# The order of the projection jobs in a streaming encoder layer

## The chip, the cores and the metric

The kernel runs as one program on 1 core of one Trainium2 chip. The metric is the device time of one execution in microseconds (us). A core has five engines that each work through a list of instructions of their own, in the order in which the list was written: PE (TensorE, matrix products), ACT (ScalarE), DVE (VectorE), POOL (GpSimd) and SP (SyncE, which in this kernel only issues DMAs). An instruction waits on semaphores until those before it on other engines, or the DMAs that it needs, are done. PEld is the loading of PE's stationary operand, which overlaps the products.

## The reference

One layer of an encoder is computed for a prompt of 2048 frames and for 64 further frames of a running stream. The layer normalizes its input of width 1024, projects it with one matrix of 4096 columns, and cuts the product into eight features of width 512:

```python
aq, ak, av, ag, hq, hf, hi, hg = jnp.split(rms_norm(x, ln_g) @ w_in, SPLITS, axis=-1)
o_a = attn_fn(heads(aq), k, v).reshape(B, T, W_A) * jax.nn.silu(ag)
o_b, S = hgrn2_branch(hq, hf, hi, hg, lb, norm_g, s0)
y = x + jnp.concatenate([o_a, o_b], axis=-1) @ w_out
```

Group A is attention over 8 heads of width 64 (query, key, value and gate: aq, ak, av, ag); each chunk of 64 frames sees itself and the 8 chunks before it. Group B is a gated linear recurrence over 4 heads of width 128 (forget gate, query, input and output gate: hf, hq, hi, hg). Keys, values and recurrent states are outputs too, and a last RMSNorm follows.

## The kernel before, in words

**Tiles and stages.** The 2112 frames are cut into four super-blocks (SUPER): 512 frames, then 512 and the 64 running ones, then 512 and 512. For each one, x is normalized and transposed into two tiles, xh (rounded) and xl (the rest), so that a product of full precision is three products of rounded operands: w's rounded part with xh, with xl, and w's rest with xh. The eight heads of group A are worked as four pairs.

**The projections are jobs.** A job is a feature of a pair or of a recurrent head: ("pq", 2) is the query of pair 2, ("hg", 0) the gate of recurrent head 0. Each super-block has 32 jobs of 128 columns of w_in; project() runs one as 24 matmuls per block of frames into one of two PSUM banks (acc), and starts an evacuation (ev_q, ev_k, ev_v or ev_v_last, ev_f, ev_i, or silu_to for the gates and the recurrent query) that brings the bank into SBUF on ACT and DVE and gives it free. The table JOBS names the order in which the main program runs the jobs, and the list `order` made from it is the order in which weights() loads their columns. The first two and the last two jobs of a super-block run in halves of the frames (x's second half can still be on its way when the first two begin). When eight jobs are left, the x tiles of the next super-block are started, or in the last super-block the loads for the output projection.

**What else is on PE.** As soon as its features are there, a pair's attention and a head's recurrence run beside the jobs of others. Attention goes s (scores, one PSUM bank), pr (softmax on DVE and ACT), tr (transposed back on PE, two banks), ph (tr split into a rounded part by ACT at L951 and a rest by DVE at L954), pv (product with the values), mixa (times the gate on POOL, L1095). A recurrence runs in one PSUM bank, g. After the last job, the steps of the output projection (out_step) fill PE; out_parts() cuts their left operands into slot, xh and xl tiles, by a copy on ACT (L1687) and a difference on POOL or DVE (L1695).

**What sets the order.** All five instruction lists are written by the Python class Plan. Every piece of work is a generator that yields what it waits for; Plan keeps a clock of its own, and whichever piece is ready first writes its instructions next. On the chip the lists are fixed: an instruction whose data are late holds up everything behind it on its engine. Buffers are counted by tokens (Tok): two for sig (staging of gates, of new key and value rows that go to the output, and of loads), three for vT (staging of query, key, value, input), two for sga (gates of pairs).

**Lines that the steps below touch.** L409 writes xh from transposed x (x_split, ACT). L645 copies transposed new rows into sig and L650 sends them to the output (new_rows). L1642 loads rows of the mixed features into the two sig and two vT buffers (out_load). L922 is the score plus bias with its minimum (DVE), L939 the softmax's exp (ACT), L942 and L943 the scaling (DVE), L1832 a square sum of the last norm (ACT), L1809 a sum of the output projection (DVE), L575 to L577 the three ACT passes of a gate.

Of the kernel before, what the change touches and what calls it, by code (L numbers as in the profile page):

```python
# [37 lines left out]
SUPER = [  # L38
# [4 lines left out]
]  # L43
NMAX = 576


JOBS = [[(k, g) for g in range(4) for k in ("hf", "hq", "hi", "hg", "pg", "pq", "pk", "pv")] for _ in SUPER]
JOBS[-1][-12:] = [("hf", 3), ("hq", 3), ("pv", 2), ("pq", 2), ("pk", 2), ("hi", 3), ("hg", 3), ("pg", 2), ("pv", 3),
                  ("pq", 3), ("pk", 3), ("pg", 3)]


class Plan:
# [131 lines left out]
def hymba_step(  # L184
# [247 lines left out]
    feature = dict(hf=20, hq=16, hi=24, hg=28, pg=12, pq=0, pk=4, pv=8)  # L432
    for sb, jobs in enumerate(JOBS):
        order += [(sb, feature[k] + g) for k, g in jobs]
# [104 lines left out]
    def project(j, ranges, evac, close=True, ready=None):  # L539
        yield lambda: j in w_at  # L540
        w, th, tl = w_at[j]
        yield th
        if ready:
            yield lambda: ready(0, 0)
        for off, bn in ranges:
            yield from tk["acc"].get()
            acc = acc_ps()
            n = 0
            for i, (wi, x) in enumerate(((0, xh), (0, xl), (1, xh))):
                for kt in range(KT):  # L550
                    if i == 2 and kt % 2 == 0:
                        yield lambda: len(tl) > kt // 2
                        yield tl[kt // 2]
                    if ready and i < 2 and kt % 4 == 0:
                        yield lambda: ready(i, kt)
                    mm(acc[:, :bn], w[:, wi, kt, :], x[:, kt, off : off + bn], bn,
                       start=(kt == 0 and i == 0), stop=(kt == KT - 1 and i == 2))
                    n += 1
                    if n % 2 == 0:
                        yield None  # L560
            C.spawn(evac(acc[:, :bn], off, bn, C.pe()), 0)
        if close:
            tk["w"].put(1, C.pe())
# [1349 lines left out]
    def program():  # L1913
# [66 lines left out]
        for sb in range(nsb):  # L1980
# [5 lines left out]
            made = {}  # L1986
            for u, (kind, g) in enumerate(JOBS[sb]):
                if u == len(JOBS[sb]) - 8:
                    if last:
# [13 lines left out]

                if u in (1, len(JOBS[sb]) - 1):
                    for half in range(2):
# [4 lines left out]
                        if u > 1:  # L2010
                            x_left[sb, half] = True
                elif u not in (0, len(JOBS[sb]) - 2):
                    yield from project(j, blocks, evac)
# [150 lines left out]
```

## Time and profile before

| | |
|---|---|
| median of 3 runs | 1251.38 us (1249.99 to 1251.63) |
| the profiled execution's own time | 1251.06 us |
| its span, first to last instruction | 1249.3 us |
| granted PE clock, mean | 0.998 |
| PE busy | 1237.7 us, 99% |
| PEld busy | 1088.6 us, 87% |
| DVE, ACT, POOL busy | 886.6, 684.4, 412.3 us |
| DMA | 287.94 MB, mean 230 GB/s |

A time is the device's for the whole execution, some 2 us more than the span. Busy time of PE comes from modelled ends, so neighbouring matmuls overlap in a listing; how long PE really took for a run of matmuls is read from the starts.

### The profile page before, as it was taken

To read this page: it belongs to the slowest core of one execution; us is meant where nothing else is said; L and a number is where in the kernel's file an instruction comes from. 1 tells how busy PE (TensorE), PEld (TensorE's weight loads), DVE (VectorE), ACT (ScalarE), POOL (GpSimd) and SP (SyncE) were. 2 spreads that over 40 slices of the span, in tenths; PEclk is the share of its full clock that TensorE was granted. 3 is DMA by queue.
4 is the path that set the end of the run, shared out by engine and by line. 5 is a ranking of instruction groups with operands and counts; after the bars stand their busy time and mean duration, and the time that the engine had idled before them with its cause. 6 is when DMAs were issued, how large, how long until landed. Compare 5 with 4: busy or idle time off the path is not lost. (4 is left out here: it accounts for less than half of the span.)

```text
span 1249.3 us, 21363 instructions
## 1 busy us (share of the span) xinstructions
PE 1237.7 (99%) x7520; PEld 1088.6 (87%) x7520; DVE 886.6 (71%) x1889; ACT 684.4 (55%) x1534; POOL 412.3 (33%) x702
## 2 busy tenths in 40 slices
PE   9999999999999999999999999999999999999997
PEld 8888888999999999998888888988888888788786
DVE  7697878866767578776576677775757476767775
ACT  6354545665656556574555566664655445643443
POOL 7666564101020111200233242133241103474543
PEclk9999999999999999999999999999999999999999
DMA  8897888666565474654777778687766655887431
GB/s 337 301 325 257 313 301 318 203 192 222 166 195 166 144 276 155 206 178 150 284 247 252 266 263 280 227 258 248 231 243 210 218 203 211 333 273 237 139 123 68
DMA packets 137956, 287.94 MB, mean 230 GB/s; under 512 B 35257, under 2 KB 79289, under 8 KB 120186
## 3 DMA queue, kind: packets, MB, share of 16 engines
q1 hardware_dynamic: 137560, 286.58, 67.6%
q8 instruction: 59, 0.97, 0.3%
q14 instruction: 47, 0.39, 0.1%
q10 hardware_dynamic: 290, 0.01, 0.0%
HBM read 195.31 MB, written 92.27 MB: 230 GB/s over the span
## 5 line engine op out<-in xcount | busy, mean ns | idle before, releaser
L249 PE MATMUL acc<-xh,w 128*128 128x512 f32 (+2 forms) x2752 | 568.6, 345 | 0.5 <-ACT xh L409 0.5
L249 PEld LDWEIGHTS acc<-xh,w 128*128 128x128 f32 x2752 | 439.3, 189 | 50.6 <-ACT xh L409 0.9
L249 PE MATMUL acc<-xl,w 128*128 128x512 f32 (+2 forms) x1376 | 294.8, 345 | 0.0
L249 PEld LDWEIGHTS acc<-xl,w 128*128 128x128 f32 x1376 | 221.1, 189 | 24.4
L939 ACT ACTIVATE pr<-pr,nm 128x640 f32<-128x640 f32 (+4 forms) x132 | 100.4, 761 | 60.0 <-DVE nm L922 59.5
L951 ACT CAST ph<-tr 128x512 fp32r<-128x512 f32 (+3 forms) x176 | 88.2, 507 | 78.5 <-PE pv L249 45.8
L922 DVE CUSTOM_DVE_ANT_0 pr<-s,bias 128x640 f32<-128x640 f32 (+4 forms) x128 | 94.2, 736 | 41.1 <-PE s L249 40.3
L473 POOL TENSOR_TENSOR w<-wraw,w 128x256 fp32r<-128x256 f32 x120 | 102.4, 884 | 55.0 <-DVE w L468 43.1
L954 DVE TENSOR_TENSOR ph<-tr,ph 128x512 fp32r<-128x512 f32 (+3 forms) x176 | 101.2, 588 | 26.3 <-ACT ph L951 25.5
L249 PE MATMUL pv<-ph,v 128*128 128x256 f32 (+2 forms) x344 | 98.6, 370 | 0.1
L253 PE MATMUL tr<-ident,pr 128*128 128x128 f32 x580 | 88.1, 273 | 1.3 <-DVE ph L954 1.3
L993 DVE TENSOR_TENSOR mixa<-mixa,pv 64x256 f32<-64x256 f32 (+1 forms) x144 | 56.9, 395 | 43.3 <-ACT mixa L989 39.7
L510 POOL TENSOR_TENSOR xn<-wraw,xn 128x256 fp32r<-128x256 f32 x48 | 39.0, 814 | 142.4 <-ACT xn L507 137.1
L1095 POOL TENSOR_TENSOR mixa<-mixa,sga 128x256 f32<-128x256 f32 (+1 forms) x36 | 27.9, 776 | 162.8 <-DVE mixa L993 152.0
L253 PEld LDWEIGHTS tr<-ident,pr 128*128 128x128 f32 x580 | 69.7, 140 | 10.9 <-issue 1.7
L943 DVE TENSOR_SCALAR pr<-pr,sm 128x640 f32<-128x640 f32 (+4 forms) x132 | 74.6, 565 | 4.7
L1532 POOL TENSOR_TENSOR k<-ob 128x512 f32<-128x512 f32 (+2 forms) x20 | 18.2, 910 | 176.0 <-ACT ob L1523 136.0
L575 ACT ACTIVATE sig<-acc 128x512 f32<-128x512 f32 (+2 forms) x64 | 32.2, 503 | 74.6 <-PE acc L249 72.0
L249 PEld LDWEIGHTS pv<-ph,v 128*128 128x128 f32 (+1 forms) x344 | 58.2, 189 | 7.3 <-issue 0.5
L989 ACT COPY mixa<-pv 64x256 f32<-64x256 f32 (+1 forms) x72 | 25.2, 350 | 64.8 <-PE pv L249 59.5
L249 PE MATMUL s<-kd,q 128*128 128x320 f32 (+2 forms) x232 | 55.8, 310 | 0.0
L249 PE MATMUL s<-kd,ql 128*128 128x320 f32 (+2 forms) x232 | 55.5, 309 | 0.0
(333 smaller groups left out, 2133.3 us busy)
## 6 DMA issues: line engine op xcount, KB each, us to landing
w<-wd SPq DMA_DIRECT2D x96, 1024.0 KB, 5.8
wd<-w SPq DMA_DIRECT2D x32, 1024.0 KB, 7.3
wraw<-in_w_in_dram SPq DMA_DIRECT2D x30, 512.0 KB, 5.3
wod<-xn SPq DMA_DIRECT2D x28, 512.0 KB, 5.5
xn<-in_x_prompt_dram SPq DMA_DIRECT2D x23, 512.0 KB, 4.6
bias<-biasd SPq DMA_DIRECT2D x24, 320.0 KB, 5.9
carry<-kd SPq DMA_DIRECT2D x12, 512.0 KB, 7.0
carry<-v SPq DMA_DIRECT2D x12, 512.0 KB, 5.5
```

What stands on the lines that cost most here:

```text
L249: pe.matmul(out, w, x, **kw)
L253: pe.transpose(out, x, idn)
L473: pool.tensor_sub(w[:, 1, k : k + 2], raw[:, k : k + 2], f32(w[:, 0, k : k + 2]))
L510: pool.tensor_sub(f32r(st[:, c.start + 512 : c.stop + 512]), src[:, c], st[:, c])
L575: act.activation(sig[:, :bn], acc, AF.Exp, scale=-1.0)
L922: dve.tensor_tensor_reduce(s[:, :nk].rearrange("p (a c) -> p a c", a=ns), sps[:, :ns, :kn], d.bias[:, h, bcol : bcol + nk].rearrange("p (a ...
L939: act.activation(s[:, :nk], s[:, :nk], AF.Exp, bias=nm[:, 0:1], scale=-1.0, accum_out=sm)
L943: dve.tensor_scalar(s[:, :nk], s[:, :nk], sm, None, ALU.mult)
L951: act.copy(ph[:krows, 0, :wid], pt[:krows, :wid])
L954: dve.tensor_sub(ph[:krows, 1, :wid], pt[:krows, :wid], f32(ph[:krows, 0, :wid]))
L993: dve.tensor_add(mix[hs, :qn], mix[hs, :qn], pv[hs, i, :qn])
L1095: pool.tensor_mul(mix[:, :n], mix[:, :n], d.sg[:, g0 : g0 + n])
```

## The change

The table JOBS is replaced. Before, each of the four turns of a super-block held the same eight kinds in one order: hf, hq, hi, hg of a head, then pg, pq, pk, pv of the pair of the same number; only the last twelve jobs of the last super-block stood apart. Now the first three super-blocks share a table EACH, in which the order inside a turn differs from turn to turn, and the last super-block has a table END, in which jobs of different pairs and heads are mixed: it opens with a query and a gate (pq 0, hg 0) in place of hf 0 and hq 0. The numbers of jobs, matmuls, loads and buffers are the same. 11 lines are added, so that L951 of before is L962 of the changed kernel.

```diff
-JOBS = [[(k, g) for g in range(4) for k in ("hf", "hq", "hi", "hg", "pg", "pq", "pk", "pv")] for _ in SUPER]
-JOBS[-1][-12:] = [("hf", 3), ("hq", 3), ("pv", 2), ("pq", 2), ("pk", 2), ("hi", 3), ("hg", 3), ("pg", 2), ("pv", 3),
-                  ("pq", 3), ("pk", 3), ("pg", 3)]
+EACH = [
+    ("hf", 0), ("hq", 0), ("hg", 0), ("hi", 0), ("pq", 0), ("pk", 0), ("pg", 0), ("pv", 0),
...
+]
+END = [
+    ("pq", 0), ("hg", 0), ("pg", 0), ("hq", 0), ("hf", 0), ("pk", 0), ("hi", 0), ("hf", 1),
...
+    ("pk", 2), ("hi", 3), ("hg", 3), ("pq", 3), ("pv", 3), ("pg", 2), ("pk", 3), ("pg", 3),
+]
+JOBS = [EACH for _ in SUPER]
+JOBS[-1] = END
```

**Place 1: PE, the first jobs of the second super-block.** tr and g here are transposes of the last x tile of the second half (xn_2708 before, xn_2707 now); acc_2899 and acc_2897 are the first matmuls that read that half from xh. Before:

```order
L253 MATMUL tr_2863<-ident_69,xn_2708 128x64 x4
L249 MATMUL acc_2824<-xh_153,w_2556 128x256 x6
L249 MATMUL s_2883<-kd_569,q_571 128x256
L249 MATMUL s_2883<-kd_569,ql_155 128x256
L253 MATMUL g_2889<-ident_69,xn_2708 128x64 x4
L249 MATMUL acc_2899<-xh_153,w_2447 128x320 x8
```

And now:

```order
L264 MATMUL tr_2853<-ident_69,xn_2707 128x64 x4
L260 MATMUL acc_2830<-xl_154,w_2503 128x256 x2
L264 MATMUL tr_2862<-ident_69,xn_2707 128x64 x4
L260 MATMUL acc_2830<-xl_154,w_2503 128x256 x2
L260 MATMUL g_2873<-q_562_2668,ones_74 128x512
L260 MATMUL g_2873<-q_563_2669,ones_74 128x512
L260 MATMUL acc_2830<-xl_154,w_2503 128x256 x2
L260 MATMUL acc_2830<-xh_153,w_2503 128x256 x8
L260 MATMUL acc_2897<-xh_153,w_2459 128x320 x2
```

Before, no row stands between the last transposes and the matmuls that read the half; now five rows do.

**Place 2: ACT and DVE, where the output projection begins.** sig_12850 (before) and sig_12843 (now) are the second of the loads of mixed features; ph_12961 and ph_12946 are the attention tiles of the last pair that stand next behind its copy into xh. ACT before:

```order
L1687 CAST slot_12859<-sig_12848 128x512
L1687 CAST xh_153<-sig_12850 128x512
L1832 ACTIVATE ck_12937,ss_12938<-xn_12024 128x512
L989 COPY mixa_12805<-pv_12806 64x256
L1687 CAST slot_12924<-wraw_12021 128x512
L939 ACTIVATE pr_12932,sm_12955<-pr_12932,nm_12933 128x640
L951 CAST ph_12961<-tr_12903 128x512
L951 CAST ph_12970<-tr_12925 128x512
```

ACT now, and behind it the DVE rows that end in the second half of the same ph:

```order
L1000 COPY mixa_12804<-pv_12805 64x256
L1698 CAST slot_12852<-sig_12841 128x512
L1698 CAST xh_153<-sig_12843 128x512
L1698 CAST slot_12934<-wraw_12018 128x512
L962 CAST ph_12946<-tr_12919 128x512
L950 ACTIVATE pr_12929,sm_12951<-pr_12929,nm_12930 128x640
L1843 ACTIVATE ck_12964,ss_12965<-xn_12021 128x512
L962 CAST ph_12991<-tr_12935 128x256
```

```order
L953 RECIPROCAL sm_12951<-sm_12951 128x1
L954 TENSOR_SCALAR pr_12929<-pr_12929,sm_12951 128x640
L933 ISA pr_12976,nm_12977<-s_12953,bias_576 128x640
L933 ISA nm_12977 128x1
L1850 TENSOR_SCALAR b_2509_12967<-ss_12965 128x1
L1820 TENSOR_TENSOR asb_79<-asb_79,acc_12938 128x512
L965 TENSOR_TENSOR ph_12946<-tr_12919,ph_12946 128x512
```

The copy of the late sig tile still stands ahead of the attention's ph; four ACT rows stood between them, now one does. On DVE the ph row stands behind the scaling of pr_12929, whose exp comes after ph on ACT.

**Place 3: PE at the same place.** acc_12964 and acc_12979 are the output step whose left operand comes from the first sig tile, acc_12988 the step that reads xh; tr_12993 and tr_13011 are transposes of pr that need a tr bank back from the ph above. Before:

```order
L249 MATMUL acc_12964<-b11h_12604,slot_12859 128x512 x2
L249 MATMUL acc_12964<-b11l_12605,slot_12859 128x512
L249 MATMUL acc_12988<-w_12495,xh_153 128x512
L249 MATMUL acc_12988<-w_12495,xl_154 128x512
L253 MATMUL tr_12993<-ident_69,pr_12799 128x128
L253 MATMUL tr_12993<-ident_69,pr_12836 128x128
L249 MATMUL pv_12969<-ph_12961,v_570 128x512 x2
```

And now:

```order
L260 MATMUL acc_12979<-b11h_12581,slot_12852 128x512 x2
L260 MATMUL acc_12979<-b11l_12582,slot_12852 128x512
L260 MATMUL s_12997<-kd_573,q_575 128x320 x2
L260 MATMUL s_12997<-kd_573,ql_155 128x320 x2
L260 MATMUL acc_12979<-b11h_12581,slot_12852 128x512 x2
L260 MATMUL acc_12979<-b11l_12582,slot_12852 128x512
L260 MATMUL acc_12979<-b11h_12581,slot_12852 128x512
L264 MATMUL tr_13011<-ident_69,pr_12894 128x128
L264 MATMUL tr_13011<-ident_69,pr_12929 128x128
```

Scores and a pv have moved into the output step, and the transposes now stand ahead of the step that reads xh. The last 453 rows of PE's list, from the output steps shortly after this place to the end, are the same in both kernels but for buffer numbers.

5 rows, old and new, of tables (EACH, END) are left out of this document.

## The prediction

> **What bounds the kernel now.** I read the page first, then PE's waits, a table of stretches, the chain that ended last, and the timelines around the longest waits. From the page:
>
> ```profile
> span 1249.3 us, 21363 instructions
> PE 1237.7 (99%) x7520; PEld 1088.6 (87%) x7520; DVE 886.6 (71%) x1889; ACT 684.4 (55%) x1534; POOL 412.3 (33%) x702
> PEclk9999999999999999999999999999999999999999
> ```
>
> PE is the bound, at a clock that is never withheld. The stretches (start and end, length; then PE, PEld, DVE, ACT, POOL busy, clock, DMA share, GB/s) show where PE stands idle at all:
>
> ```profile
> 12.00:200.00 188.00, 188.00 (x1022) 158.94 (x1022) 147.75 (x283) 95.98 (x202) 118.56 (x169) 1.00 0.87 309
> 200.00:420.00 220.00, 219.42 (x1643) 210.13 (x1641) 158.37 (x421) 126.79 (x310) 35.35 (x108) 1.00 0.60 197
> 420.00:640.00 220.00, 220.00 (x1501) 203.02 (x1500) 154.71 (x375) 127.05 (x298) 37.86 (x99) 1.00 0.62 209
> ```
>
> Nothing in the first and third, 0.58 us where the second super-block starts. PE's waits, by who ended them (us in total, times, longest):
>
> ```profile
> PE pv L1962 <- POOL one L279: 1.4, 1, 1.4
> PE tr L253 <- DVE ph L954: 1.3, 1, 1.3
> PE acc L249 <- DVE pr L1783: 0.6, 1, 0.6
> PE acc L249 <- ACT xh L409: 0.5, 1, 0.5
> PE acc L249 <- DVE xn L1783: 0.4, 1, 0.4
> PE acc L249 <- POOL slot L1695: 0.3, 1, 0.3
> PE acc L249 <- DVE slot L1695: 0.3, 1, 0.3
> ```
>
> Seven waits, 4.8 us. The change gives PE the same instructions in another order, so at best it removes the waits that it reaches. The first is the program's start; the two on L1783 and the one on DVE slot lie in the last 453 PE rows, which are alike in both kernels. Three are left: xh, slot on POOL, and ph. Busy ends on PE are modelled, so what each costs is read from starts, against the price of a matmul that waits for nothing. That price is in the chain that ended last:
>
> ```profile
> 1102.50 18.72 PE acc L249 x82
> ```
>
> 82 matmuls of 512 columns in 18.72 us: 0.228 each. [...]
>
> **The change part by part.** *The second super-block's start (place 1).* PE, then ACT's cast, with start, length and what:
>
> ```profile
> 239.75 1.12 PE L249 MATMUL acc<-xh,w 128*128 128x256 f32 x8
> 240.71 1.12 PE L249 MATMUL acc<-xl,w 128*128 128x256 f32 x8
> ...
> 244.79 0.85 PE L249 MATMUL acc<-xh,w 128*128 128x320 f32 x4
> 246.13 0.85 PE L249 MATMUL acc<-xh,w 128*128 128x320 f32 x4 [0.49 <-ACT xh L409]
> 246.82 0.33 PE L249 MATMUL s<-kd,q 128*128 128x384 f32 x1
> ```
>
> ```profile
> 245.72 0.35 ACT L409 CAST xh<-g 128x256 fp32r<-128x256 f32 x1
> ```
>
> The first four 320-column matmuls on the last half of x started 1.34 us before the next four, which took 0.69 (246.13 to 246.82). So 0.65 us was lost, to a cast that ACT ran only at 245.72, behind a gate's passes. Before, those matmuls stand right behind the last transposes of that half. Now ten 256-column matmuls of the other half (8 in 0.96 us by the rows, 0.12 each) and two of 512 columns stand there first: 10 x 0.12 + 2 x 0.228 = 1.66 us, more than the 0.65 lost. The wait goes unless ACT comes 1.0 us later than it did. What is late next is nothing in this stretch: the row of the next one shows 220.00 busy of 220. Gain 0.65; bounds: 0 (ACT's queue is also reordered) and 0.65.
>
> *The rest of the first three super-blocks.* Turns get another order, and each order changes which gate, key or value is evacuated when. There PE waits 0.09 us beside the above (0.58 less 0.49), so nothing can be gained, and any cover that gets too thin costs. The thinnest is in attention: transposed scores go through ACT and DVE before pv can use them.
>
> ```profile
> L951 ACT CAST ph<-tr 128x512 fp32r<-128x512 f32 (+3 forms) x176 | 88.2, 507 | 78.5 <-PE pv L249 45.8
> L954 DVE TENSOR_TENSOR ph<-tr,ph 128x512 fp32r<-128x512 f32 (+3 forms) x176 | 101.2, 588 | 26.3 <-ACT ph L951 25.5
> L939 ACT ACTIVATE pr<-pr,nm 128x640 f32<-128x640 f32 (+4 forms) x132 | 100.4, 761 | 60.0 <-DVE nm L922 59.5
> ```
>
> The two take 507 + 588 ns = 1.10 us. Counted over PE's lists at the prices above, the nearest pv stands 2.48 us of PE work behind its transposes before, and 2.08 now. That leaves 0.98 us in hand in place of 1.38: one softmax pass (0.76) that ACT has ahead is still covered, a second (1.52 together) opens a wait of 0.54. Bounds for such waits: 0, and 1.35 each (the ph wait below, the longest of the kind in the trace). I take 0.3 us in all, the size of the shortest waits listed, because only one place is that tight.
>
> *Where the output projection begins (places 2 and 3).* The chain:
>
> ```profile
> 1069.39 5.59 DMA out_dram<-sig
> ...
> 1083.36 0.69 DVE ph L954
> ```
>
> The two sig buffers take turns: new rows to the output, the gate's passes, new rows again (5.59, to 1074.98), then the load of mixed rows, which ACT meets at 1078.76. PE, ACT and DVE behind it:
>
> ```profile
> 1078.92 0.62 PE L249 MATMUL acc<-b11h,slot 128*128 128x512 f32 x2
> ...
> 1080.28 0.39 PE L249 MATMUL acc<-b11h,slot 128*128 128x512 f32 x1
> 1080.94 0.50 PE L249 MATMUL acc<-b11h,slot 128*128 128x512 f32 x1 [0.27 <-POOL slot L1695]
> ...
> 1082.45 0.39 PE L249 MATMUL acc<-w,xl 128*128 128x512 f32 x1
> 1084.19 0.41 PE L253 MATMUL tr<-ident,pr 128*128 128x128 f32 x2 [1.35 <-DVE ph L954]
> ```
>
> ```profile
> 1078.76 0.62 ACT L1687 CAST xh<-sig 128x512 fp32r<-128x512 f32 x1 [2.42 <-DMA sig<-mixd]
> 1079.29 0.63 ACT L1832 ACTIVATE ck<-xn 128x512 bf16<-128x512 f32 x1
> ...
> 1080.30 0.62 ACT L1687 CAST slot<-wraw 128x512 fp32r<-128x512 f32 x1
> 1080.82 0.83 ACT L939 ACTIVATE pr<-pr,nm 128x640 f32<-128x640 f32 x1
> ...
> 1081.77 1.07 ACT L951 CAST ph<-tr 128x512 fp32r<-128x512 f32 x2
> ```
>
> ```profile
> 1075.54 0.16 DVE L942 RECIPROCAL sm<-sm 128x1 f32<-128x1 f32 x1
> 1075.74 0.55 DVE L943 TENSOR_SCALAR pr<-pr,sm 128x640 f32<-128x640 f32 x1
> 1076.21 0.81 DVE L922 CUSTOM_DVE_ANT_0 pr<-s,bias 128x640 f32<-128x640 f32 x1
> ...
> 1081.22 0.67 DVE L1809 TENSOR_TENSOR asb<-asb,acc 128x512 f32<-128x512 f32 x1
> ```
>
> Start to start, 0.66 instead of 0.23 was lost to POOL's slot (0.43), and 1.74 instead of 0.23 to ph (1.51): 1.94 us. ACT stood 2.42 us for the sig tile, with square sum, slot, exp and ph queued behind it.
>
> Now the slot: six scores and products (two pv of 0.228 and four s of 0.147, an estimate between the 0.12 of 256 columns and the 0.228 of 512) have moved into that output step, 1.04 us, so POOL's 0.43 is covered. The ph: its ACT half moves up, its DVE half doesn't, since the scaling of an exp that now follows ph on ACT stands ahead of it on DVE. Worked through with the same starts: xh 1078.76, slot 1079.29, ph 1079.81 (0.52 on, 1080.30 to 1080.82), exp 1080.34 (half of 1.07), its end with the sum's read 1081.29 (0.95, 1080.82 to 1081.77); then DVE's reciprocal 0.20 (1075.54 to 1075.74), scaling 0.47 (1075.74 to 1076.21), score 0.81, a one-column scalar 0.16 like the reciprocal's own length, a sum 0.67 and ph 0.69: 1084.29, about as late as before (1083.36 + 0.69 = 1084.05). PE's position: the step on the first sig tile begins 0.9 us of work later in the new list, 1079.8, and 12 matmuls and four s (2.74 + 0.59) stand before the transposes that want the bank: 1083.1. A wait of 1.1 to 1.2 us stays; I take 1.1, since listed lengths run past the next start. Gain 1.94 - 1.1 = 0.84; bounds 0 (DVE later by as much) and 1.94 (the load lands 1.1 earlier, because a gate's turn came sooner).
>
> *Moved loads.* The columns of w_in are loaded in the jobs' order, so each load moves with its job; the first super-block, where DMA is busiest (0.87 share), has PE 188.00 busy of 188, and its first two jobs stay. Cost nothing; if that cover were gone, a weight would be late by part of a load.
>
> **The sum.** -0.65 - 0.84 + 0.3 = -1.2 us. The profiled execution took 1251.06, its span 1249.3; so 1249.9 for such an execution. The median of the runs lies 0.3 above the profiled one: 1251.38 - 1.2 = 1250.2. The difference is under 0.2% (2.5 us), about what a measurement of this kernel can tell from no change.
>
> **The rivals.** *A: all waits go.* If the sig load comes a microsecond earlier and no cover gets thin, 0.65 + 1.94 = 2.6 us: 1248.8; with the 0.09 of the stretch and a smaller wait in the tail, 1248.6. For it: the reached waits are exactly these. Against it: DVE's order still puts the scaling ahead of ph. It is on the edge of what can be told. 0.24.
>
> *B: slower, one more DMA turn in the sig chain.* The gate of pair 2 now comes three jobs later, and its staging is a sig buffer that new value rows need next.
>
> ```profile
> L575 ACT ACTIVATE sig<-acc 128x512 f32<-128x512 f32 (+2 forms) x64 | 32.2, 503 | 74.6 <-PE acc L249 72.0
> ```
>
> Between its last matmul and the transposes of those rows lie 8.9 us of PE work; its three ACT passes (503 ns for the first kind) and a product on DVE take some 2.1. If ACT is held by a sig load for over 6.8 us, the new rows wait, and the next copy and load start a turn of 5.59 us later, which PE meets at ph: 1250.2 + 4.5 to 5.6, about 1255. Against it: ACT's longest wait for a sig load here is 2.42. 0.07. [...]
>
> *C: given back in attention.* If the tight place gets two softmax passes ahead of it, 0.54 opens in each of four pairs of three super-blocks where it recurs, at most 6.5 us, and four of them (2.2) already outweigh the gain, seven (3.8) carry it past +0.2%: 1251 to 1255, since 1250.2 with 2.2 to 6.5 less the 0.3 counted. It decides from the second pass on. For it: ACT is only 55% busy, but its passes come in bursts. Against it: the kernel before has 1.38 in hand and not one such wait. 0.12, half of it above +0.2%.
>
> The forecast itself: 0.57.
>
> **How the numbers follow.** Faster by over 0.2% is A: 0.24. Slower is B and half of C, 0.13. The same is the forecast and the rest of C, 0.63. The range: low end 1248.2, A with the spread of the runs taken off (0.4 below); high end 1253.0, the forecast with both gains at their lower bounds (1251.4), plus one longest wait of 1.35, and C's smaller cases. Left out are B, the upper half of C, and the spread of A below.
>
> **What would show it.** Right: no wait on xh L409's line at about 245 us; none on POOL slot at about 1080; a wait for DVE's ph of about 1 us at about 1084; PE busy at 220.00 in the middle stretches. A: no wait on ph either. B: a third output DMA in the chain ahead of the load, and a PE wait of over 4 us. C: waits on ph or pr at several places between 250 and 1070 us. Wrong altogether: a PE whose 512-column price leaves 0.228, or a clock below 9 in a slice; then the order acts through something that the waits don't hold.

## The result, and the profile after

| | before | changed kernel |
|---|---|---|
| median of 7 runs | 1250.81 us | 1254.44 us (1252.72 to 1256.16) |
| ratio to before, 95% interval | | 1.0029 (1.0018 to 1.0041) |
| the profiled execution, its span | 1251.06, 1249.3 | 1254.22, 1252.5 |
| first to last start on PE | 1240.85 | 1243.36 |

The change makes the kernel 0.29% slower, 3.6 us, where 1.2 us of gain were forecast. In the two profiled executions 2.5 us of the 3.2 us between the spans lie in PE's list; the other 0.7 us lie behind PE's last start. There the two executions agree up to the issue of the last output DMA, 3.96 us behind that start; it lands 2.08 us later before and 2.73 us later now. Of the other ten profiled executions of this study nine have 2.1 and one, that of the run with the first table alone, 2.9. The run with gi on POOL has the changed kernel's list on PE and 2.1, so this part is not PE's order; why the transfer varies is open.

The page of the changed kernel, then PE's waits (us in total, times, longest):

```profile
span 1252.5 us, 21367 instructions
PE 1238.4 (99%) x7520; PEld 1088.7 (87%) x7520; DVE 895.2 (71%) x1890; ACT 681.4 (54%) x1533; POOL 413.2 (33%) x702
PEclk9999999999999999999999999999999999999999
```

```profile
PE s L260 <- DVE nm L933: 2.1, 3, 1.6
PE pv L1973 <- POOL one L290: 1.4, 1, 1.4
PE s L260 <- DVE kd L815: 0.9, 1, 0.9
PE g L260 <- ACT k L1485: 0.6, 1, 0.6
...
PE acc L260 <- DVE xl L426: 0.2, 1, 0.2
```

PE is still the bound, with the same instructions and the same clock (0.998 in the mean in both). Every wait that the prediction said could go is gone: none on xh, none on POOL's slot, none on ph. The three rows left out are those of the last 453 rows of PE's list (0.6, 0.4 and 0.2; before 0.6, 0.4 and 0.3). But these are new: scores s waiting for DVE (nm, kd), a recurrence's g waiting for ACT's k, and a small one on xl. The stretches show where. Before, then now; the columns are those of the prediction's table:

```profile
0.00:60.00 60.00, 58.57 (x329) 49.45 (x330) 39.09 (x68) 30.75 (x62) 41.10 (x71) 1.00 0.90 330
240.00:260.00 20.00, 19.51 (x147) 18.74 (x146) 16.17 (x53) 13.92 (x40) 2.00 (x9) 1.00 0.74 239
260.00:300.00 40.00, 40.00 (x311) 38.61 (x310) 25.82 (x65) 22.03 (x55) 5.61 (x20) 1.00 0.63 198
1040.00:1084.00 44.00, 42.57 (x263) 36.90 (x261) 29.24 (x65) 25.19 (x55) 17.60 (x22) 1.00 0.75 276
```

```profile
0.00:60.00 60.00, 57.45 (x314) 47.79 (x315) 43.15 (x77) 30.91 (x66) 42.17 (x71) 1.00 0.86 317
240.00:260.00 20.00, 20.00 (x151) 19.42 (x150) 16.07 (x50) 17.04 (x49) 3.82 (x14) 1.00 0.72 250
260.00:300.00 40.00, 37.78 (x283) 36.20 (x282) 24.78 (x63) 19.31 (x47) 2.10 (x3) 1.00 0.61 198
1040.00:1084.00 44.00, 43.67 (x280) 38.99 (x279) 34.73 (x71) 28.72 (x64) 17.20 (x21) 1.00 0.76 254
```

PE loses 1.1 us of busy time in the first 60 us and 2.2 us between 260 and 300, and wins 0.5 and 1.1 us at the two places of the prediction.

A finer account follows from starts. Each kind of pair of neighbouring matmuls (told apart by the tiles they write and their shapes) gets one price for both kernels (the mean start-to-start time of such a pair, without its slowest tenth); what a kernel takes beyond the prices is summed along its list. The changed kernel's sum less that of before, at points of the list (us of priced work; the prices sum to some 1207):

```
work done        20    60   140   220   260   300   320   640  1020  1040  1060  1220
after - before  0.3   1.3   2.0   1.7   1.1   4.7   4.6   4.7   4.6   5.0   3.0   3.1
```

Two steps up before 150, one down near 240, a large one up between 260 and 300, no lasting one for 700 us, and one down at 1040 to 1060. The time comes and goes at single places; no turn of jobs has a price of its own.

**The largest new place.** PE, ACT and DVE of the changed kernel where the second super-block's first pair begins its attention:

```profile
287.79 0.71 PE L260 MATMUL g<-gi,k 128*128 128x128 f32 x4 [0.64 <-ACT k L1485]
...
292.90 1.42 PE L260 MATMUL acc<-xh,w 128*128 128x256 f32 x10
295.88 0.56 PE L260 MATMUL s<-kd,q 128*128 128x320 f32 x2 [1.56 <-DVE nm L933]
```

```profile
285.94 0.62 ACT L623 CAST wraw<-ck 128x512 fp32r<-128x512 f32 x1 [3.04 <-DMA ck<-in_cache_attn_v_dram]
286.58 0.46 ACT L790 CAST q<-vT 64x320 fp32r<-64x320 f32 x1
287.06 0.40 ACT L812 CAST kd<-vT 64x256 fp32r<-64x256 f32 x1
287.38 0.36 ACT L1485 COPY k<-g 128x256 f32<-128x256 f32 x1
...
289.70 0.43 ACT L805 COPY vT<-acc 128x320 f32<-128x320 f32 x1 [1.54 <-PE acc L260]
293.48 0.61 ACT L1290 COPY gi<-vT 128x256 f32<-128x256 f32 x2 [3.35 <-DMA vT<-way]
293.99 0.45 ACT L812 CAST kd<-vT 64x320 fp32r<-64x320 f32 x1
```

```profile
294.48 0.48 DVE L815 TENSOR_TENSOR kd<-vT,kd 64x320 fp32r<-64x320 f32 x1 [3.91 <-ACT kd L812]
294.99 0.82 DVE L933 CUSTOM_DVE_ANT_0 pr<-s,bias 128x640 f32<-128x640 f32 x1
```

Read it backwards. The scores at 295.88 want the one bank of s; DVE empties it at 294.99, behind its half of the key at 294.48; that needs ACT's half at 293.99; and ACT stood 3.35 us in front of it, in the copy of a recurrent head's input (gi), which waits for a DMA round trip. The key itself had been in SBUF since a copy by ACT at 289.70 us. So a DMA that the scores do not need held them for 1.7 us. At 287 it is the same picture with the cached values' load: ACT waits 3.04 us, and k's copy stands three rows behind it.

The jobs make the wait at 294 us: in the new first turn hi is followed at once by pq and pk; before, hg and pg stood between. The waits of ACT and DVE for these DMAs, in the kernel before and in the changed one:

```profile
ACT gi L1279 <- DMA vT<-way: 5.1, 3, 2.8
DVE w L468 <- DMA wraw<-in_w_in_dram: 0.7, 2, 0.4
```

```profile
ACT gi L1290 <- DMA vT<-way: 11.7, 8, 3.3
DVE w L479 <- DMA wraw<-in_w_in_dram: 5.1, 2, 3.6
```

### The profile page after: what moved, and what is told of

Its sections match the earlier page's. It is cut to its first block, busy times and chain, and to the rows that moved or that the text cites. A ratio compares the mean times of both kernels' runs of the same rounds, so it can differ in the third digit from the quotient of the medians.

```text
span 1252.5 us, 21367 instructions
## 1 busy us (share of the span) xinstructions
PE 1238.4 (99%) x7520; PEld 1088.7 (87%) x7520; DVE 895.2 (71%) x1890; ACT 681.4 (54%) x1533; POOL 413.2 (33%) x702
## 5 line engine op out<-in xcount | busy, mean ns | idle before, releaser
L260 PE MATMUL acc<-xl,w 128*128 128x512 f32 (+2 forms) x1376 | 291.3, 344 | 0.2 <-DVE xl L426 0.2
L962 ACT CAST ph<-tr 128x512 fp32r<-128x512 f32 (+3 forms) x176 | 87.9, 507 | 71.2 <-PE pv L260 33.8
L954 DVE TENSOR_SCALAR pr<-pr,sm 128x640 f32<-128x640 f32 (+4 forms) x132 | 81.4, 617 | 4.7
L260 PEld LDWEIGHTS pv<-ph,v 128*128 128x128 f32 (+1 forms) x344 | 58.5, 189 | 7.7 <-DVE v L674 0.5
```

Of the source, the lines that this page charges most:

```text
L260: pe.matmul(out, w, x, **kw)
L954: dve.tensor_scalar(s[:, :nk], s[:, :nk], sm, None, ALU.mult)
L962: act.copy(ph[:krows, 0, :wid], pt[:krows, :wid])
```

## The experiments

Theory Q (queue): the lost time is that of a few evacuations that stand in ACT's or DVE's list behind an instruction that waits for a DMA. Rival D (distance): the new order puts the scores too close behind the key's matmuls, whatever stands in the queues. Rival S (spread): the new order costs a little in each turn. Medians are of 5 or 11 runs, beside runs of the kernel before on the same chip (medians 1250.4 to 1250.9).

**gi's copies on POOL.** All other lists keep their order, PE's and DVE's word for word:

```diff
-                    act.copy(r.iv[:rows, off + c : off + c + w].rearrange("p (t a j) -> p a t j", a=4, j=32),
+                    pool.tensor_copy(r.iv[:rows, off + c : off + c + w].rearrange("p (t a j) -> p a t j", a=4, j=32),
```

> The changed kernel, its lists on PE and DVE word for word the same; only the 24 copies of a head's input into gi (which wait for a DMA round trip) are taken from ACT and given to POOL. Theory Q (queue: in the new first turn the key's cast on ACT stands behind a gi copy that waits 3.3 us for its DMA): the 1.72 us that PE loses at 294 us goes, the waits at 287 (0.8, behind another DMA) and 51 us (1.1, on DVE) stay; 1254.4 - 1.7 = 1252.7. Theory D (distance: the new order puts the scores too close behind the key's matmuls for any queue): the wait at 294 us stays, 1254.4. Theory S (spread: the new order costs a little in every turn): 1254.4.

Measured: 1254.03, ratio 1.0026 (1.0017 to 1.0034). The copy now waits on POOL, and at the former 294 us the scores wait for nothing:

```profile
294.89 0.46 PE L260 MATMUL s<-kd,q 128*128 128x320 f32 x2
```

```profile
294.18 0.90 POOL L1290 COPY gi<-vT 128x256 f32<-128x256 f32 x2 [10.73 <-DMA vT<-way]
```

From 260 to 320 us of work the kernel loses 1.6 us against before, where the changed kernel lost 3.4. PE's list is the same, so D falls for this wait. The time by itself does not say so: the median moved by 0.4 us, not by 1.7, Q's 1252.7 lies outside the interval, and the 1254.4 of D and S inside. The profiled execution is one of the faster ones (1253.17); PE's list is 0.7 us shorter in it than in the changed kernel's. There the wait at 51 us was 0.4 longer, and one of 0.5 stood at 117 us, which another run has too (0.5 in the one with the first table alone, where nothing moves to POOL).

**The cached values' split on POOL as well.**

```diff
-        act.copy(dh, s4)
+        pool.tensor_copy(dh, s4)
...
-        dve.tensor_sub(v[:rows, t0 : t0 + nt, 1:3, :], s4, f32(dh))
+        pool.tensor_sub(v[:rows, t0 : t0 + nt, 1:3, :], s4, f32(dh))
```

> The changed kernel with gi's copies on POOL as in the first run, and also both halves of the split of the cached values (wraw from ck, which wait for a DMA on ACT and then on DVE) on POOL; PE's list is word for word that of the changed kernel. Theory Q: the wait of g at 287 us (0.8 to 0.9) goes too, since k's copy no longer stands behind a DMA on ACT; the sum of the waits from 280 to 300 us, 3.1 in the changed kernel and about 1.2 with gi on POOL, falls under 0.3. Time about 0.8 below the run with gi alone: 1253.2. Theory D (distance in PE's list): 287 us keeps its wait, 1254.

Measured: 1252.46, ratio 1.0015 (1.0006 to 1.0024). The waits of g on k and of the scores near 290 us are gone from PE's list of waits. The sum of that stretch is 1.4, not under 0.3, since two smaller waits came up just behind it (0.5 at 295 us, on a row of q from DVE; 0.2 at 297 us).

**And the cast of one weight.** The ninth job's weight arrives in the first super-block by a load of its own; its cast stood on DVE ahead of the first key's second half:

```diff
-            dve.tensor_copy(w[:, 0], raw)
+            (pool if j == 8 else dve).tensor_copy(w[:, 0], raw)
```

> As the run before it, and the one cast of a weight at 50 us (the ninth job's, which waits for its load on DVE ahead of the key's second half) on POOL. PE's list is still that of the changed kernel. Theory Q: the wait of s at 51 us (1.1 to 1.5) goes as well; what is left over the kernel before is then about 1 us of small waits, against the 2.7 us that the changed order saves: about 1250.5, at or a little below the kernel before. Theory D or a spread cost: 1253 to 1254.

Measured: 1252.62, ratio 1.0014 (1.0005 to 1.0022). At 51 us, in the changed kernel (DVE, PE), and then in this one (POOL, PE):

```profile
50.58 0.69 DVE L479 CAST w<-wraw 128x1024 fp32r<-128x1024 f32 x1 [1.49 <-DMA wraw<-in_w_in_dram]
51.31 0.69 DVE L815 TENSOR_TENSOR kd<-vT,kd 64x512 fp32r<-64x512 f32 x1
52.05 0.33 PE L260 MATMUL s<-kd,q 128*128 128x128 f32 x1 [0.93 <-DVE kd L815]
```

```profile
50.03 1.04 POOL L479 CAST w<-wraw 128x1024 fp32r<-128x1024 f32 x1 [1.01 <-DMA wraw<-in_w_in_dram]
50.74 0.22 PE L260 MATMUL s<-kd,q 128*128 128x128 f32 x1
```

The load is still late, and the cast waits for it, but the scores no longer do. The median did not follow. In the profiled execution what was won there is given back at 117 us: PE is done with the matmuls ahead of a recurrence's transposes 1.1 us earlier than in the changed kernel, but DVE is not. Its seven us of work ahead of them begin behind POOL (fq), at 109.22 us here and at 108.83 in the changed kernel.

```profile
116.86 0.66 PE L264 MATMUL g<-ident,bl 128*128 128x128 f32 x4 [0.90 <-DVE asb L1474]
```

In the changed kernel PE waits for nothing there: a wait removed early in the program can be lost again at a later thin cover. (In the run with six moved rows below, 0.3 us is lost there.)

**The control: the kernel before with the same three moves.**

> A control: the kernel before with the same three moves to POOL; its PE list is word for word that of before. Theory Q: the kernel before has no wait at these places, so nothing is gained: 1250.9, within 0.7. If a lighter ACT and DVE by itself made these kernels faster, this one would be 2 to 3 us below before.

Measured: 1252.8, ratio 1.0011 (1.0002 to 1.002). Lightening ACT and DVE wins nothing; it costs 0.11%, with new waits such as 0.8 us at 123 us. Against this control, the changed order with the same moves is level (1.0014 against 1.0011): with the three blocks gone, the order costs nothing that can be told.

**Only the instructions at the three places.** Six rows of lists move: the gi copies of head 0 in the second super-block, the split of pair 0's cached values, and the one cast.

```diff
+                    (pool.tensor_copy if (sb, h) == (1, 0) else act.copy)(r.iv[:rows, off + c : off + c + w]
...
+        (act.copy if p else pool.tensor_copy)(dh, s4)
+        (dve if p else pool).tensor_sub(v[:rows, t0 : t0 + nt, 1:3, :], s4, f32(dh))
```

> The changed kernel with only six instructions moved to POOL, all at the three places: gi's copies of the first head and the two halves of the cached values' split in the second super-block (three copies and two halves), and the cast of the ninth job's weight. PE's list is that of the changed kernel. Theory Q: from 260 to 320 us it loses under 1.3 against the kernel before where the changed kernel lost 3.4, and nothing at 51 us; without the small waits that the wide moves brought to the kernel before (0.9 by 120 us), 1250.4, within 0.1% of the kernel before. If the three places aren't the cause, 1253 to 1254.4.

Measured: 1251.74, ratio 1.0009 (1.0 to 1.0018): 0.20 of the 0.29% are back, 2.7 us between the medians, with PE's list untouched. In the profiled executions PE's list is 1.9 us shorter than in the changed kernel, of the 2.5 it had lost; 0.65 more is the last output DMA, which lands in 2.08 us again. Its stretches:

```profile
0.00:60.00 60.00, 58.52 (x321) 49.24 (x322) 43.30 (x77) 31.35 (x66) 43.44 (x72) 1.00 0.88 327
260.00:300.00 40.00, 39.53 (x300) 38.23 (x299) 26.04 (x68) 21.05 (x49) 5.98 (x13) 1.00 0.65 207
```

PE is back to 58.5 of 60 and 39.5 of 40. From 260 to 320 us of work it loses 1.4 us against before; under 1.3 was expected. What is left over the kernel before are small waits, the largest of 0.7 us at 479 and 0.6 us at 294 us. In this execution the weight's load had come early (its cast waited for POOL, until 49.26, and not for the DMA), so the place at 51 us rests on the run before.

**The first three super-blocks' table alone.**

```diff
-JOBS = [EACH for _ in SUPER]
-JOBS[-1] = END
+JOBS = [EACH, EACH, EACH, OLD_LAST]
```

> The new table for the first three super-blocks, the old one for the last. Theory Q: the five new waits up to 300 us come (0.3 + 1.1 + 0.9 + 1.3 + 2.1, less 0.6 at 245 us and 0.2 around it: 4.8 us), the tail keeps its 1.9; 1250.8 + 4.8 = 1255.6. Theory S: three quarters of the 3.6 us of the whole change, 1253.5.

Measured: 1258.16, ratio 1.0061 (1.0047 to 1.0074). The waits at 51, 287 and 294 us came again (0.7, 1.0, 1.5 by starts). Up to 1040 us of work it loses 4.7, as the changed kernel does (5.0). The rest, 2.6 us in sum, was not foreseen, and neither number is met: the planner had written the old tail anew, and two waits on xn stand in it.

```profile
PE acc L262 <- DVE xn L1796: 2.5, 2, 2.1
```

**The last super-block's table alone.**

```diff
+JOBS = [OLD, OLD, OLD, END]
```

> The old order in the first three super-blocks, the new table in the last. Theory Q: only the tail changes: both waits of 1080 to 1084 us go (1.9), a new one at 1065 us (0.4) may come; 1250.8 - 1.8 = 1249.0 with it counted partly. Theory S: a quarter of 3.6 us, 1251.7.

Measured: 1252.25, ratio 1.0008 (1.0 to 1.0017). Q's 1249.0 lies outside the interval, S's 1251.7 inside. But the trace shows a single place and no spread: the tail's two waits at 1080 us are gone, but a new one takes as much, and it is not a DMA's: transposes of a value wait for a bank, whose last reader stands on DVE behind 1.8 us of a query's evacuation.

```profile
1063.78 0.44 PE L266 MATMUL tr<-ident,vT 128*128 128x128 f32 x2 [1.74 <-DVE v L845]
```

```profile
1061.46 0.94 DVE L795 TENSOR_TENSOR ql<-vT,q 64x512 fp32r<-64x512 f32 x1
1062.41 0.85 DVE L796 CAST q<-q 64x512 fp32r<-64x512 f32 x1
1063.30 0.42 DVE L845 TENSOR_TENSOR v<-tr,v 128x256 fp32r<-128x256 f32 x1
```

**That wait taken away,** by the last super-block's second casts of queries on POOL, with PE's and ACT's lists the same:

```diff
-                dve.tensor_copy(d.q[own[1 - h], h, c], f32(d.q[own[h], h, c]))
+                (pool if last else dve).tensor_copy(d.q[own[1 - h], h, c], f32(d.q[own[h], h, c]))
```

> The old order in the first three super-blocks and the new table in the last, as in the run with that table alone (1252.25), with the last super-block's second casts of the queries on POOL; PE's list is that of the table alone. Theory Q: PE's 1.9 us at 1062 us (transposes of a value behind 1.8 us of a query's evacuation on DVE) falls to about 1.0 or less, and the tail keeps its gain: 1251.0, no more than 0.5 below the kernel before. If the lost time there was another wait, 1252.3.

Measured: 1251.24, ratio 1.0003 (0.9994 to 1.0012); the wait fell to 0.9, and the median by 1.0. This is the best version with a part of the change in it, and it cannot be told from the kernel before. No version tried beats both kernels.

**The old order with hg ahead of hi in the first turn, and the new last table.**

> The old order with one edit in the first three super-blocks (hg before hi in the first turn), and the new table in the last. Theory Q: the pair's gate stands again between a head's input and the pair's query and key, so no wait at 51, 287 and 294 us; the wait of 0.65 at 245 us goes as in the changed kernel; with the tail's 1.8: 1250.8 - 2.4 = 1248.4. Theory S: under one us slower than before, 1251.5. Theory D: as Q, because the distance is the old one.

Measured: 1257.22, ratio 1.0048 (1.0036 to 1.0061): a miss for every theory as I had put it. The waits at 51 and 294 us stay away, as Q and D both say. The wait on xh at 245 us, which I had put down to hg's place in the turn, stays. And the cached values' split now stands in DVE's list ahead of a recurrence's state, its load came late, and PE waits longer than at any place before:

```profile
288.86 0.62 ACT L627 CAST wraw<-ck 128x512 fp32r<-128x512 f32 x1 [4.29 <-DMA ck<-in_cache_attn_v_dram]
...
289.51 0.69 DVE L630 TENSOR_TENSOR wraw<-ck,wraw 128x512 fp32r<-128x512 f32 x1 [5.36 <-ACT wraw L627]
...
290.90 0.49 PE L264 MATMUL g<-asb,gi 128*128 128x128 f32 x2 [2.87 <-DVE stp L1520]
```

The mechanism is Q's, at another place; my expectation had asked only whether the old places came back. In the tail 1.9 us is lost at 1068 us, to transposes of a value as in the run with the last table alone.

**hi a job earlier in the changed kernel's first turn.**

```diff
-    ("hf", 0), ("hq", 0), ("hg", 0), ("hi", 0), ("pq", 0), ("pk", 0), ("pg", 0), ("pv", 0),
+    ("hf", 0), ("hq", 0), ("hi", 0), ("hg", 0), ("pq", 0), ("pk", 0), ("pg", 0), ("pv", 0),
```

> The changed kernel with hi ahead of hg in the first turn (hf, hq, hi, hg, pq, pk, pg, pv), so the DMA round trip of hi starts a job earlier. Theory Q: the wait at 294 us goes or falls under 0.4, since a job of 24 matmuls of 256 to 320 columns is about 3.2 us and ACT stood 3.35 us; the waits at 51 us and 287 us, behind other DMAs, may stay: 1252.5. Theory D: the key is where it was, the wait stays: 1254.4.

Measured: 1255.87, ratio 1.0043 (1.0031 to 1.0056). The wait at 294 us goes, as Q says and D denies, although the key stands where it stood; 287 goes too: from 260 to 320 us of work 0.4 is lost in place of 3.4. The planner then writes the rest anew, and two waits that have nothing to do with that place cost more than was saved:

```profile
PE pv L260 <- DVE mixa L1004: 1.9, 1, 1.9
PE tr L264 <- DVE v L843: 1.8, 1, 1.8
```

## Why the prediction was wrong

**The bound: right.** PE stays at 99%, the clock at 9 in all slices, and 2.5 of the 3.2 us between the profiled spans are PE's waits. By starts 2.8 us was the ceiling of the gain, and all of it was in fact won: 0.65 at 245 us, 0.25 at 204 (by busy times, in the prediction, 0.09), 1.9 at 1080 to 1084.

**Place 1: right,** in mechanism and size. No wait on xh, and the sum falls by 0.6 between 220 and 260 us of work. By the rows of place 1 twelve 256-column matmuls stand in between, not ten, so the cover is 1.9 us and not 1.66. ACT's last cast also came early, at 244.73; PE read it from 246.63 on.

**Places 2 and 3: right in direction, mis-sized.** 0.84 was forecast, 1.9 came (from 5.0 to 3.1 in the sum), less 0.5 for a new wait at 1065 us. The term that failed is the wait of 1.1 us that was to stay. I had taken the chain of sig buffers over from the trace of before. Its slow link there was the first write of new rows, which landed only 6.0 us after its issue:

```profile
1061.11 6.01 DMA out_dram<-sig
```

The second half of the last gate (that of pair 3, the last job in both kernels) waited for that buffer. Now the same write, issued at 1065.92, lands in 2.5 us, and the gate waits for PE alone (before, then now):

```profile
1067.20 0.39 ACT L575 ACTIVATE sig<-acc 128x256 f32<-128x256 f32 x1 [1.89 <-DMA out_dram<-sig]
```

```profile
1069.36 0.39 ACT L586 ACTIVATE sig<-acc 128x256 f32<-128x256 f32 x1 [0.43 <-PE acc L260]
...
1080.48 0.62 ACT L1698 CAST xh<-sig 128x512 fp32r<-128x512 f32 x1
```

So the last copy of new rows leaves 5.7 us behind the first (1065.92 and 1071.58) and no longer 8.3 (1061.11 and 1069.39). ACT's xh starts 3.5 us ahead of PE's step on the first sig tile (1083.98), where before it started 0.16 us ahead (1078.76 and 1078.92), and no wait on ph is left. The time of that write goes with the last super-block's table: 6.0 and 6.2 us in the kernel before and the control, 2.3 to 2.8 us in all nine profiled runs with the new last table, 3.5 with the first table alone. Why it lands sooner is open.

**The step that failed: "The thinnest is in attention: transposed scores go through ACT and DVE before pv can use them ... I take 0.3 us in all".** No wait on ph came at all. I looked for the thinnest cover in the work that stands between two PE rows, and priced ACT and DVE by their busy times. The cover that broke is that of the evacuations ahead of the scores and of the recurrence, and at the largest places what used it up is not work: ACT or DVE stood idle in front of an instruction that waited for a DMA, with the evacuation queued behind it. By starts, the new waits are 1.1 (51 us), 0.8 (287), 1.7 and 0.3 (288 to 294), 0.4 (20), 0.4 (139), 0.2 (80) and 0.5 (1065): 5.4 us where 0.3 stood in the sum. 5.4 less the 2.8 won is 2.6, PE's 2.5 us. The first four, 3.9 us, stand behind a DMA in this way. At the other four, 1.5 us, DVE worked without a pause, and the evacuation that PE wanted stood behind work of others in its list; that part no run took away by itself.

**"Moved loads ... Cost nothing": wrong at one place,** and not because the load moved with its job. The ninth job is hf of head 1 in both tables. Its load was issued at 45.31 us, before at 43.08, because four writes of hi's round trip now stand ahead of it in SP's list (41.09 to 45.21), and it landed at 50.46, before at 49.13. The cover named was PE's busy time in the first super-block. DVE's queue was not looked at: the cast that waits for that load now has the key's second half right behind it, since the key comes a job earlier, and PE lost 1.1 us. Before, the key's half ran only at 59.59.

**The rivals.** A came half: all reached waits went, but new ones came. B did not, as said; the gate of pair 2 comes two jobs later, not three, and its passes (from 1053.50) wait for PE alone. C was right in kind, given back beside attention, and nearly in size; its mechanism, two softmax passes ahead of ph, did not show, and its places were to lie between 250 and 1070 us, where the trace has them at 20 to 295 us for the most part. The time lies above the range because C's upper half was left out of it. (With both gains at nothing the forecast is 1251.7, not 1251.4; with one wait of 1.35 that gives the stated 1253.0.)

What in the trace of before could have told it: the two rows of ACT's and DVE's waits for DMAs shown above, and this one. Before, too, ACT waits as long for the cached values:

```profile
288.43 0.62 ACT L612 CAST wraw<-ck 128x512 fp32r<-128x512 f32 x1 [2.86 <-DMA ck<-in_cache_attn_v_dram]
```

PE did not feel it, because what stood behind it then was wanted only later: the copy of k ran at 294.49, six us on. For each such instruction in the new lists, the question is what stands behind it and how soon PE reads that.

## What to carry to other kernels

When an order of work changes in a kernel whose busiest engine never rests, list the instructions on the other engines that wait for a DMA, and read in the new lists what is queued right behind each one and when the busy engine wants it; the busy times of those engines do not show it. An instruction that waits for a DMA belongs on an engine whose next work nobody waits for soon: here six such moves brought back 0.20 of 0.29%. And where a planner writes the lists, the parts of a reordering do not add up: the two tables alone gave +0.61% and +0.08%, together +0.29%, since each edit rewrites what stands behind it.

## What the runs showed of the hardware

- One small transfer took a multiple of its usual time. In the changed kernel the 32 KB read of the round trip that ends at gi took 7.2 us at 286 us, issued behind a 1024 KB load of weights and a 128 KB read; the median of this kernel's reads of that size is 2.1 us (eight reads, of which the trace has the landing of six):

```profile
vT<-way SPq DMA_DIRECT2D x1, 32.0 KB, 7.2
```

```profile
vT<-way SPq DMA_DIRECT2D x8, 32.0 KB, 2.1
```

- One wait behind a DMA differed from run to run with the lists up to it unchanged. PE's loss at 51 us was 1.1 us in the changed kernel, 1.5 with gi on POOL, 0.4 with the cached values on POOL too and 0.7 with the first table alone, though the lists of all engines are alike up to that place in these four. One profile shows such a wait, but not its size.
- With gi on POOL, two copies of gi pieces of 256 columns took 0.90 us on POOL (from 294.18); on ACT, in the changed kernel, two took 0.61 us (from 293.48).
